# MLP "up" phases: the first group's plain halves and sums behind the copy of the second group's first product

## The chip, the cores and the metric

The kernel runs on one core of a Trainium2 chip. The metric is device time in microseconds for one execution. TensorE (PE) does the matmuls, VectorE (DVE) and ScalarE (ACT) the elementwise work, GpSimd (POOL) some elementwise work and accumulating DMAs, SyncE (SP) issues most loads.

## The reference

An encoder of two layers over 512 positions of width 1024: a stick-breaking attention, a squared-relu MLP, a gated linear recurrence, and a second MLP, each on a normed input and added to the stream. The change lies in both MLPs:

```python
def squared_relu_mlp(h, w1, w2):
    u = jax.nn.relu(h @ w1)
    return (u * u) @ w2          # w1: 1024 x 4096, w2: 4096 x 1024

x = x + squared_relu_mlp(rms_norm(x, norm_mlp[layer]), mlp_w1[layer], mlp_w2[layer])
```

## The kernel before, in words

Every matmul in full precision is made of three in a faster format: an operand is split into a high half (a cast, on ScalarE: `wh`, `bh`, `sh`) and a low half (operand minus high half, on VectorE: `wl`, `bl`, `sl`), and high by high, high by low and low by high are summed in PSUM.

The MLP is cut into four quarters of the hidden width. Each quarter is an "up" phase (input to hidden) and a "down" phase (hidden to output). Each phase multiplies 2 x 2 blocks by Strassen's scheme in Winograd's form: seven products `P1` to `P7` instead of eight, with sums of blocks before and after. The first quarter's up part is done directly (`squared`); the other three go through `run`, so `run` holds three up phases in each MLP, six in all.

An up phase has 14 steps of PE: the seven products for group `p = 0` and then the seven for `p = 1`, in the order P1 P5 P6 P3 P7 P2 P4 (`UP`). A group is one half of the quarter's hidden columns. P1, P6 and P7 add up in one PSUM bank, so the bank after P1 must be copied out before P6 may write it again; P5 and P3 share a second bank. After each step, `leave` writes the work on its product: copies of partial sums, combinations, relu and square. It also prepares operands of PE four steps ahead (`prepare`, `make`, `operand`): a cast `wh` and a subtraction `wl` for each weight block, and before some of them a sum `b` of two blocks, done on VectorE or by an accumulating DMA.

The hidden values of a group are four blocks, `u[0]` to `u[3]`. For the down phase they are needed as they are ("plain") and in four sums (`sums`), and each of these as halves (`split`). For group 0 the halves go to `bh` and `bl`; for group 1 to `sh` and `sl`. Plain halves of group 0 cover blocks 0 to 2 in one instruction of 1536 elements a partition; four `sums` of 512 elements overwrite the `u` blocks; the halves of the sums follow in two instructions of 1024.

ScalarE and VectorE execute this code in the order it is written: each is wrapped in `Ordered`, which ties every instruction to the one before it. Line 765 of the profile is the line of that wrapper, so instructions have to be told apart by their tiles. PE's order is written by hand as well. DMA queues are placed by the scheduler.

Of the kernel before, what the change touches and what calls it, by code (L numbers as in the profile page):

```python
# [61 lines left out]
def hybrid_encoder(  # L62
# [712 lines left out]
    class Mlp:  # L775
# [333 lines left out]
        def run(self, first, between, end):  # L1109
# [13 lines left out]
            def place(i):  # L1123

                return (i + self.STEPS // 2) % self.STEPS
# [35 lines left out]
            def prepare(i):  # L1161

                if i < len(steps) and steps[i][0] == "up":

                    if steps[i][3] == "P7" or self.layer and steps[i][1:] == (1, 0, "P4"):
                        return
                if i - 1 in range(len(steps)) and i - 1 not in made and i > 2:
                    make(i - 1)
                if i < len(steps) and steps[i][0] == "down":
                    add(i, 0)  # L1170
                    if waiting and place(i) in (20, 22, 23):
                        self.split_slot(*waiting.pop(0))
                make(i)
                for n in range(i + 1, i + 6):
                    add(n, n - i)

            def last_sums(u, which):
                for to, a, b, how in which:
                    self.V.tensor_tensor(u[to], u[a], u[b], how)
# [23 lines left out]
            def leave(i):  # L1203

                ahead = i + 4
                if i < 0:
                    return
                kind, q4, p, name = steps[i]
                bank = sums[kind, q4, p if kind == "up" else 0][self.PRODUCTS[name][3]]
                if kind == "down":  # L1210
                    if p:
                        for n in range(2):
                            self.collect(name, n, bank[n])
                    prepare(ahead)
                    if q4 == 0:

                        k = {19: 2, 20: 2, 24: 3, 25: 3}.get(place(i))
                        if k:
                            (self.sums_of_x if place(i) in (19, 24) else self.halves_of_sums)(k)
                        if place(i) == 26:  # L1220
                            self.replace()
                    return
                u, three = us[p], bank.rearrange("p (i n) -> p i n", i=2)
                keep = {"P1": 0, "P6": 1, "P5": 2, "P7": 3}.get(name)
                if keep is not None:

                    self.A.copy(u[keep], three)
                at, x, y, op = {
                    "P3": (1, three, u[1], ALU.subtract),
                    "P7": (2, u[2], u[3], ALU.subtract),  # L1230
                    "P2": (0, u[0], three, ALU.add),
                    "P4": (3, three, None, None),
                }.get(name, (None,) * 4)
                if op:
                    self.V.tensor_tensor(u[at], x, y, op)
                if name == "P4":
                    self.A.activation(u[3], three, AF.Relu)
                    self.square(u[3])
                    if p:
                        last_sums(u, self.SUMS[:2])  # L1240
                if later:
                    later.pop()()
                prepare(ahead)
                if op:
                    def rest(u=u, at=at):
                        self.A.activation(u[at], u[at], AF.Relu)
                        self.square(u[at])
                        if p:
                            self.split_slot(p, u[at], at)

                    if p and name == "P3":
                        later.append(rest)
                    else:
                        rest()
                    if name == "P2" and not p:
                        self.split(p, slice(0, 2), slice(0, 3), slice(0, 3))
                elif name == "P4" and p:
                    last_sums(u, self.SUMS[2:3])
                    self.split_slot(p, u[2], 5)
                    last_sums(u, self.SUMS[3:])  # L1260
                    waiting[:] = [(p, u[j], 3 + j) for j in (0, 1, 3)]
                elif name == "P4":
                    self.sums(p, slice(0, 2))
                elif name in ("P5", "P6") and p:
                    n = ("P5", "P6").index(name)
                    self.split(0, n, slice(0, 4), slice(3, 7))
# [16 lines left out]
            for i, (kind, q4, g, name) in enumerate(steps):  # L1283
                load(i)
                leave(i - 1)
                if i == len(steps) - 2:
                    break
                if kind == "down":
                    self.part(sums.setdefault((kind, q4, 0), {}), name, g, ws.pop(i))
                    continue  # L1290
                if name == "P1":
                    us[g] = self.slots_of(g)
                banks = sums.setdefault((kind, q4, g), {})
                to = self.PRODUCTS[name][3]
                new = to not in banks
                if new:
                    banks[to] = self.bank()
                self.up(name, ws.pop(i), banks[to], new)
# [492 lines left out]
```

## Time and profile before

| | |
|---|---|
| runs | 1038.54, 1039.32, 1039.6 us; median 1039.32 |
| profiled execution | 1039.46 us, of which the span of instructions is 1037.8 |
| PE | 1026.1 us busy, 99% |
| VectorE | 858.9 us, 83% |
| ScalarE | 701.8 us, 68% |
| GpSimd | 172.3 us, 17% |
| granted TensorE clock | 0.998 |

Times in rows of the profile are us from the start of the span: start, duration, engine, line, operation, what is written and read. `[1.48 <-ACT bh L765]` at the end of a row says that the engine was idle for 1.48 us before it, until the instruction named ended. Consecutive rows of one engine overlap by some 0.1 us, since a row ends when its last write is acknowledged. The six up phases run through `run` begin at 329, 407, 485, 796, 876 and 954 us; one takes some 39 us, as does a down phase.

### The profile page before, as it was taken

Reading aid. Unit: us, or ns where it says so; the run is one execution under the profiler, and the core shown is the slowest. Engines: PE = TensorE matmul, PEld = TensorE weight load, DVE = VectorE, ACT = ScalarE, POOL = GpSimd, SP = SyncE. Lnnn points to the kernel's source line nnn. Section 1 sums busy time; section 2 is a strip of 40 time slices with the busy share of each in tenths; the row PEclk is TensorE's granted clock in tenths of the full one; section 3 lists DMA queues with packets and bytes.
Section 4 is the critical chain, followed back from the end, with each engine's and each line's share of the span. In section 5 each row is a group of like instructions: output and inputs, shape, how many; then the busy total and the mean of one; then the engine's idle time right before and its main releaser. Section 6 shows DMA issues by size and latency. Waiting matters only on the chain.

```text
span 1037.8 us, 15857 instructions
## 1 busy us (share of the span) xinstructions
PE 1026.1 (99%) x5862; PEld 897.0 (86%) x5862; DVE 858.9 (83%) x1148; ACT 701.8 (68%) x1083; POOL 172.3 (17%) x239
## 2 busy tenths in 40 slices
PE   9999999999999999999999999999999999999997
PEld 7888888888888988988988888888888988988986
DVE  6888787847888898898899888984789798898897
ACT  6777676826766773773775799964755773873866
POOL 0444344420010010010011121200010010010013
PEclk9999999999999999999999999999999999999999
DMA  7745454528546677667682575462446677677654
GB/s 238 214 120 143 115 152 103 160 91 294 142 78 189 185 134 206 172 132 208 163 206 79 151 191 144 102 223 87 96 73 177 176 146 198 161 149 196 159 123 111
DMA packets 53260, 160.46 MB, mean 155 GB/s; under 512 B 6720, under 2 KB 8256, under 8 KB 53184
## 3 DMA queue, kind: packets, MB, share of 16 engines
q1 hardware_dynamic: 42096, 120.35, 35.4%
q0 software_dynamic: 10656, 38.80, 23.1%
q8 instruction: 46, 0.75, 0.3%
q10 hardware_dynamic: 432, 0.31, 0.1%
q14 instruction: 30, 0.25, 0.1%
HBM read 137.41 MB, written 4.19 MB: 136 GB/s over the span
## 4 chain that ended last, share of the span: by engine, by line
PE 74%; DVE 10%; issue 7%; ACT 5%; DMA 3%; POOL 0%; POOLq 0%; DVEq 0%; ACTq 0%
PE ps_t L1071 10%; PE ps_acc L1071 5%; PE ps_acc L231 5%; PE ps_acc L229 5%; PE ps_acc L230 5%; PE ps_acc L976 5%; DVE wl L765 4%; PE ps_z L976 4%; PE ps_t L229 2%; PE ps_t L231 2%; PE ps_t L230 2%; PE ps_z L1071 2%; ACT wh L765 2%; PE ps_o L976 2%; PE ps_o L229 2%
## 5 line engine op out<-in xcount | busy, mean ns | idle before, releaser
L765 ACT CAST wh<-b 128x1024 fp32r<-128x1024 f32 x168 | 174.2, 1049 | 125.0 <-DVE b L765 77.6
L765 DVE TENSOR_TENSOR wl<-b,wh 128x1024 fp32r<-128x1024 f32 x168 | 203.7, 1220 | 46.8 <-ACT wh L765 46.4
L1053 POOL DMA_DIRECT2D b<-in_w_dn x40 | 35.0, 874 | 364.5 <-DVE b L765 269.9
L229 PE MATMUL ps_acc<-xgh,wh 128*128 128x512 f32 x192 | 78.5, 409 | 0.0
L231 PE MATMUL ps_acc<-xgl,wh 128*128 128x512 f32 x192 | 75.2, 392 | 0.0
L230 PE MATMUL ps_acc<-xgh,wl 128*128 128x512 f32 x192 | 75.1, 391 | 0.0
L224 DVE TENSOR_TENSOR wl<-raw,wh 128x512 fp32r<-128x512 f32 (+2 forms) x70 | 62.0, 912 | 14.5 <-ACT wh L222 14.3
L589 DVE TENSOR_TENSOR_SCAN scan<-keep,later 128x128 f32<-128x128 f32 (+1 forms) x64 | 59.5, 934 | 17.0 <-ACT keep L579 11.5
L765 ACT ACTIVATE u<-u 128x512 f32<-128x512 f32 x100 | 63.1, 633 | 7.4 <-DVE u L765 5.9
L222 ACT CAST wh<-raw 128x512 fp32r<-128x512 f32 (+2 forms) x70 | 50.7, 759 | 20.8 <-PE ps_acc L231 7.3
L593 POOL TENSOR_TENSOR w<-w,scan 128x128 f32<-128x128 f32 (+1 forms) x64 | 51.7, 809 | 57.2 <-DVE scan L589 54.0
L1053 POOL DMA_DIRECT2D b<-in_w_up x24 | 20.8, 868 | 238.5 <-DVE b L765 71.2
L765 DVE TENSOR_TENSOR b<-b,b 128x1024 f32<-128x1024 f32 x48 | 58.7, 1223 | 1.3
L765 DVE TENSOR_TENSOR u<-u 128x512 f32<-128x512 f32 (+1 forms) x92 | 54.8, 596 | 2.7 <-ACT u L765 1.1
L765 ACT CAST wh<-raw 128x1024 fp32r<-128x1024 f32 x46 | 48.1, 1048 | 8.4 <-PE ps_acc L1071 8.3
L976 PE MATMUL ps_z<-xgh,wh 128*128 128x256 f32 x192 | 53.7, 280 | 0.0
L976 PE MATMUL ps_z<-xgh,wl 128*128 128x256 f32 x192 | 53.7, 280 | 0.0
L976 PE MATMUL ps_acc<-low,wh 128*128 128x256 f32 x192 | 53.6, 279 | 0.0
L1071 PE MATMUL ps_t<-wl,sh 128*128 128x512 f32 x126 | 49.8, 395 | 1.0 <-DVE wl L765 0.9
L1071 PE MATMUL ps_t<-wh,bh 128*128 128x512 f32 x126 | 49.2, 391 | 0.0
L1071 PE MATMUL ps_t<-wh,sl 128*128 128x512 f32 x126 | 49.2, 390 | 0.0
L1071 PE MATMUL ps_t<-wl,bh 128*128 128x512 f32 x126 | 49.1, 390 | 0.0
(399 smaller groups left out, 3416.7 us busy)
## 6 DMA issues: line engine op xcount, KB each, us to landing
b<-in_w_dn SPq DMA_DIRECT2D x48, 512.0 KB, 4.5
b<-in_w_dn POOLq DMA_DIRECT2D x40, 512.0 KB, 5.7
b<-in_w_up SPq DMA_DIRECT2D x36, 512.0 KB, 4.6
b<-in_w_up POOLq DMA_DIRECT2D x24, 512.0 KB, 5.6
raw<-in_w_m SPq DMA_DIRECT2D x16, 512.0 KB, 4.3
raw<-in_w_dn SPq DMA_DIRECT2D x16, 512.0 KB, 4.6
raw<-in_w_in SPq DMA_DIRECT2D x16, 512.0 KB, 3.8
raw<-in_w_qk SPq DMA_DIRECT2D x12, 512.0 KB, 3.6
```

Source lines behind the costliest of these rows:

```text
L222: A.copy(wh[:, k, :], raw[:, k, :])
L224: V.tensor_tensor(wl[:, k, :], raw[:, k, :], f(wh[:, k, :]), ALU.subtract)
L229: PE.matmul(ps, wh, ah, start=start, stop=False)
L230: PE.matmul(ps, wl, ah, start=False, stop=False)
L231: PE.matmul(ps, wh, al, start=False, stop=stop)
L589: V.tensor_tensor_scan(sc[:, S - n : S][:, ::-1], keep[:, :n][:, ::-1], later[:, S - n :][:, ::-1], 1.0, ALU.mult, ALU.max,)
L593: G.tensor_tensor(wt, wt, sc[:, S - n + 1 : S + 1], ALU.mult)
L765: ins = getattr(self.e, name)(*args, **kwargs)
L976: PE.matmul(ps[:, i * HS : (i + 1) * HS], m, y, start=new and i == k == n == 0, stop=i == 1 and k == C // 2 - 1 and n == 2, skip_group_che ...
L1053: G.dma_start(out=unit[b].rearrange("p j n -> p (j n)"), in_=unit["src"](to), accum_op=ALU.add)
L1071: PE.matmul(ps, m, y[:, jj, cols], start=first and n == 0, stop=last and n == 2, skip_group_check=not new,)
```

## The change

Two pieces of the work on group 0 are moved into `leave` for the first product of group 1. The plain halves (`split` of blocks 0 to 2, a cast on ScalarE and a subtraction on VectorE) stood behind relu and square of P2 of group 0, the sums behind P4 of group 0. Both now stand behind the copy of P1 of group 1.

```diff
                     else:
                         rest()
-                    if name == "P2" and not p:
-                        self.split(p, slice(0, 2), slice(0, 3), slice(0, 3))
                 elif name == "P4" and p:
...
                     waiting[:] = [(p, u[j], 3 + j) for j in (0, 1, 3)]
-                elif name == "P4":
-                    self.sums(p, slice(0, 2))
+                elif name == "P1" and p:
+                    self.split(0, slice(0, 2), slice(0, 3), slice(0, 3))
+                    self.sums(0, slice(0, 2))
                 elif name in ("P5", "P6") and p:
                     n = ("P5", "P6").index(name)
                     self.split(0, n, slice(0, 4), slice(3, 7))
```

ScalarE's order, in the first of the six up phases, from the weight half before group 0's relu of P2 to the weight half for P7 of group 1. `u<-ps_acc` is the relu of P4 of group 0, the next row its square, `wh<-b_3785` a weight for P3, `u<-ps_z` the copy of P1 of group 1 and `u<-ps_o` that of its P5:

```order
 L765 CAST wh<-b_3729 128x1024
 L765 ACTIVATE u<-u 128x2x256 x2
+L765 ACTIVATE u<-ps_acc 128x2x256
+L765 ACTIVATE u<-u 128x2x256
+L765 CAST wh<-b_3785 128x1024
+L765 COPY u<-ps_z 128x512
 L765 CAST bh<-u 128x2x768
-L765 ACTIVATE u<-ps_acc 128x2x256
-L765 ACTIVATE u<-u 128x2x256
-L765 CAST wh<-b_3785 128x1024
-L765 COPY u<-ps_z 128x512
 L765 COPY u<-ps_o 128x512
```

The cast `bh` has moved behind four instructions, to between the copies of P1 and P5.

VectorE's order at the same place. `u<-u,ps_z` is the combination for P2 of group 0, `wl<-b_3785` the low half of the weight for P3 of group 1, `u<-u x4` the four sums, `wl<-b_3783` the low half for P7 of group 1:

```order
 L765 TENSOR_TENSOR u<-u,ps_z 128x2x256
 L765 TENSOR_TENSOR wl<-b_3729,wh 128x1024
+L765 TENSOR_TENSOR wl<-b_3785,wh 128x1024
 L765 TENSOR_TENSOR bl<-u,bh 128x2x768
-L765 TENSOR_TENSOR wl<-b_3785,wh 128x1024
 L765 TENSOR_TENSOR u<-u 128x2x256 x4
 L765 TENSOR_TENSOR wl<-b_3783,wh 128x1024
```

The subtraction `bl` has moved behind one `wl`; the sums stand where they stood in the row. The other five up phases show the same two exchanges.

## The prediction

> **What bounds the kernel now.** I read the page first, then the waits of TensorE (PE), then the timeline of ScalarE (ACT) and VectorE (DVE) around one of the six places that the change touches, then PE's rows there. Two lines of the page and PE's longest waits:
>
> ```profile
> PE 1026.1 (99%) x5862; PEld 897.0 (86%) x5862; DVE 858.9 (83%) x1148; ACT 701.8 (68%) x1083; POOL 172.3 (17%) x239
> b<-in_w_dn POOLq DMA_DIRECT2D x40, 512.0 KB, 5.7
> ...
> PE ps_z L976 <- ACT u L765: 1.5, 1, 1.5
> PE ps_t L1071 <- DVE wl L765: 0.9, 3, 0.5
> ```
>
> PE is busy for 99% of the span, so there is little to win: its two longest sorts of wait in the MLPs together are 2.4 us. The question is therefore whether PE has to wait for something new. One of its waits, 1.5 us for the copy `u` on ScalarE, lies at the place of the change; the three for `wl`, the low half of a weight block, lie half a phase later.
>
> The change acts once in each of six "up" phases (three quarters after the first, in two MLPs). ScalarE there, in the first of them:
>
> ```profile
> 349.01 1.29 ACT L765 ACTIVATE u<-u 128x512 f32<-128x512 f32 x2
> 350.33 1.48 ACT L765 CAST bh<-u 128x1536 fp32r<-128x1536 f32 x1
> 351.72 0.59 ACT L765 ACTIVATE u<-ps_acc 128x512 f32<-128x512 f32 x1
> 352.34 0.63 ACT L765 ACTIVATE u<-u 128x512 f32<-128x512 f32 x1
> 352.88 1.03 ACT L765 CAST wh<-b 128x1024 fp32r<-128x1024 f32 x1
> 353.81 0.58 ACT L765 COPY u<-ps_z 128x512 f32<-128x512 f32 x1
> 354.84 0.59 ACT L765 COPY u<-ps_o 128x512 f32<-128x512 f32 x1 [0.45 <-PE ps_o L976]
> 355.33 1.05 ACT L765 CAST wh<-b 128x1024 fp32r<-128x1024 f32 x1
> ```
>
> In order: relu and square of P2; `bh`, the high plain halves of the first group (the cast that moves); relu and square of P4; a weight's high half; the copy of the second group's P1 (ps_z), then of its P5 (ps_o). VectorE beside it:
>
> ```profile
> 349.14 1.23 DVE L765 TENSOR_TENSOR wl<-b,wh 128x1024 fp32r<-128x1024 f32 x1 [0.57 <-ACT wh L765]
> 351.84 1.76 DVE L765 TENSOR_TENSOR bl<-u,bh 128x1536 fp32r<-128x1536 f32 x1 [1.48 <-ACT bh L765]
> 353.94 1.23 DVE L765 TENSOR_TENSOR wl<-b,wh 128x1024 fp32r<-128x1024 f32 x1 [0.34 <-ACT wh L765]
> 355.08 2.86 DVE L765 TENSOR_TENSOR u<-u 128x512 f32<-128x512 f32 x4
> 357.86 1.22 DVE L765 TENSOR_TENSOR wl<-b,wh 128x1024 fp32r<-128x1024 f32 x1
> ```
>
> The reader is to see that VectorE stands idle twice before the four sums (1.48 and 0.34 us), and not at all behind them. How full it stays up to the down phase, and what its few waits there are:
>
> ```profile
> 358.00:386.00 28.00, 27.92 (x168) 24.68 (x168) 26.52 (x30) 20.29 (x28) 3.54 (x5) 1.00 0.68 150
> 365.39 1.23 DVE L765 TENSOR_TENSOR b<-b,b 128x1024 f32<-128x1024 f32 x1
> 366.65 1.05 ACT L765 CAST wh<-b 128x1024 fp32r<-128x1024 f32 x1 [0.44 <-DVE b L765]
> 369.58 0.69 DVE L765 TENSOR_TENSOR sl<-u,sh 128x512 fp32r<-128x512 f32 x1 [0.62 <-ACT sh L765]
> 374.05 1.42 DVE L765 TENSOR_TENSOR u<-u 128x512 f32<-128x512 f32 x2 [0.18 <-ACT u L765]
> 383.22 2.00 ACT L765 CAST wh<-b 128x1024 fp32r<-128x1024 f32 x2 [5.33 <-DVE b L765]
> 384.30 2.36 DVE L765 TENSOR_TENSOR wl<-b,wh 128x1024 fp32r<-128x1024 f32 x2 [0.57 <-ACT wh L765]
> ```
>
> VectorE is busy for 26.52 of these 28 us. Of the 1.48 us left, 0.62, 0.18 and 0.57 are waits for ScalarE, which in turn had waited for VectorE's own sum `b` (0.44 and 5.33 us). Such waits are no slack: when VectorE comes later, ScalarE comes later, and the wait comes later with the same length. The chain ends at PE, on the second matmul of the down phase's P6, in five of the six phases:
>
> ```profile
> 351.82 0.28 PE L976 MATMUL ps_o<-s,wh 128*128 128x256 f32 x1
> 360.42 0.28 PE L976 MATMUL ps_z<-xgh,wl 128*128 128x256 f32 x1
> ...
> 385.12 0.39 PE L1071 MATMUL ps_t<-wh,sh 128*128 128x512 f32 x1
> 385.59 0.50 PE L1071 MATMUL ps_t<-wl,sh 128*128 128x512 f32 x1
> 463.27 0.50 PE L1071 MATMUL ps_t<-wl,sh 128*128 128x512 f32 x1 [0.17 <-DVE wl L765]
> 541.50 0.51 PE L1071 MATMUL ps_t<-wl,sh 128*128 128x512 f32 x1 [0.51 <-DVE wl L765]
> 822.85 0.38 PE L976 MATMUL ps_z<-bh,wh 128*128 128x256 f32 x1 [1.49 <-ACT u L765]
> 854.00 0.50 PE L1071 MATMUL ps_t<-wl,sh 128*128 128x512 f32 x1 [0.25 <-DVE wl L765]
> ...
> 928.90 0.39 PE L1071 MATMUL ps_t<-wh,bh 128*128 128x512 f32 x1
> 931.62 0.39 PE L1071 MATMUL ps_t<-wh,sh 128*128 128x512 f32 x1
> 931.95 0.50 PE L1071 MATMUL ps_t<-wl,sh 128*128 128x512 f32 x1
> ```
>
> Undisturbed, the 12 matmuls of this shape in a step take 2.72 us (928.90 to 931.62), 0.23 us each. Here the second one comes 0.47 us behind the first at 385.59 and 0.33 at 931.95, and three rows name `wl` outright. So PE takes this low half as soon as it is there: the slack is nought in these five, and I assume it nought in the sixth, whose down phase has another order. That is what decides my forecast: PE looks saturated, but through this stretch VectorE sets its pace.
>
> **The change part by part.** *The cast `bh` goes behind the copy.* It removes 1.48 us ahead of the relu of P4, so relu, square, weight half and copy begin earlier. The relu needs nothing of the cast; allowing for the overlap of neighbours of about 0.1 us (351.84 less 351.72 against a cast that ends at 351.81), it starts near 350.22. From the rows' starts: relu to square 0.62, square to `wh` 0.54, `wh` to copy 0.93. The copy starts at 352.31, 1.50 us earlier than at 353.81. The product is ready for it: the next product, P5 into ps_o, began at 351.82, so P1's last matmul began 0.12 us before and ended, with 0.28 us, near 351.98. PE's P6, which adds to that bank, may then start sooner. The list of PE's waits has one there in all six phases, the 1.49 us at 822.85.
>
> *The subtraction `bl` goes behind one `wl`.* VectorE's row order changes by that one exchange; the four sums stand where they stood, between the same neighbours, since no weight is prepared between the two places in the code. But they now follow `bl` directly, and they overwrite what `bl` reads. Their start: copy 352.31, plus 0.49 (a copy to its neighbour, 354.84 to 355.33) gives the cast at 352.80; plus 1.51 (350.33 to 351.84) gives `bl` at 354.31; plus its 1.76 and 0.02 for the hand-over gives the sums at 356.09. Before, they began at 355.08. **They begin 1.01 us later**: the copy has been put into the chain (0.49), and `bl` stands in it (1.78) in place of a `wl` (1.14) and of waits that fell away. The work that could hide this is the idle time behind the sums, and there is none but the waits that move along. So `wl` for P7, P2, P4 and those of the down phase all come 1.01 us later.
>
> *At PE.* In the first phase P7 wants its `wl` at 360.42; it now ends at 357.86 + 1.22 + 1.01 = 360.09, still in time. Further on the margin is used up, until at 385.59 it is nought, and the whole 1.01 us is PE's. PE then leads by nothing and VectorE catches up behind P6, where PE's row of waits shows none; so the next phase starts afresh and pays again. In the phase of 822.85 the wait of 1.49 goes, but the wait at 854.00 shows that PE is held by `wl` later in the same phase all the same: the time saved at P6 is spent at P7, where the `wl` is a microsecond later and PE a microsecond and a half sooner. It pays 1.01 as well.
>
> *Price of the copy by a page.* The Trainium skill, "ScalarE: Activation LUTs" (What ACT_TABLE_LOAD costs), puts an ACTIVATE with immediate operands at 186 ns and 0.833 ns an element, overlapping by 93 ns with its neighbour. Taken over to this copy of 512, as an estimate, that is 0.52 us where the rows give 0.49; the sum would be 0.2 us longer by it.
>
> *DMAs.* The written order of SyncE's queue shifts a reload of `x` and a load of the final scale ahead of one weight load each, near the ends of the MLPs' last down phases; both are read much later, and I price that at nought. Loads and accumulating DMAs that follow a `wl` or `b` of this stretch are issued 1.01 us later too. Those of GpSimd land after 5.7 us in the page's row, and feed P7 and P4, the ends of their phase; I price them at nought, and up to 0.1 us for each phase if that cover were gone.
>
> **Sum.** Six phases by 1.01 us: 6.06 us. The profiled execution took 1039.46 us (1037.8 of span and 1.66 around it), 0.14 above the median of the runs, 1039.32. Its time becomes 1045.5, and the median **1045.4 us**. Bounds for a phase: 0.5 us, if half of a delay is caught up by waits that I call fixed; 1.35 us, with 0.11 for each of two or three further interrupted steps (the matmul behind an interrupted one is late by about that: 0.50 for its duration in the rows instead of 0.39) and the DMAs. Six times these are 3.0 and 8.1: 1042.3 to 1047.4.
>
> **Rivals.**
>
> *Faster: the wait for the copy is what counts.* The mechanism is the bank of the second group's P1, which P6 adds to. Copied 1.5 us earlier it takes away 822.85's 1.49 us, the restart of 0.1 to 0.2 behind it, and a few tenths in the others: 1.8 us, and 1037.5 us. It decides if VectorE can make good 1 us between 358 and 386. For it: it is PE's longest wait in the list. Against it: 26.52 of 28 us busy, and the five rows at P6. The Trainium skill, "PSUM — Partial Sum Buffer" (Summary: rules for kernel authors), says to evacuate promptly, which is what the change does and would make it faster by this amount. The trace bears out that a late copy stops PE, once in six.
>
> *Absorbed: VectorE catches up in part.* If the waits of 0.62, 0.18 and 0.57 us were slack after all, 1.37 us would cover the 1.01 in each phase, and only the gain of one wait and the odd interrupted step would be left: within a microsecond or two, 1038 to 1041. Against it: ScalarE's rows with their own waits on VectorE's `b`. If only some phases absorb, 1041 to 1043.
>
> *Slower still: later weights delay DMAs.* Were a load late by a full step (2.72 us) in one phase of each MLP, that adds 5.4 us: 1050.8. Against it: none of PE's longest waits in the list is on a DMA.
>
> *The change does nothing* is excluded by the orders of both engines, which differ at all six places.
>
> **How the numbers follow.** Forecast with its bounds, 0.82; absorbed in full or in part, 0.09, about half of it within 0.2% (2.1 us, about what a measurement of this kernel tells from no change); faster, 0.06; slower still, 0.03. The range 1042.3 to 1047.4 is the forecast's own, and leaves out the rivals, 0.18. Faster by over 0.2%: 0.06. Within: 0.06. Slower: 0.88.
>
> **What would show it.** Right: in the timeline of ScalarE the copy of the second group's P1 stands before `bh`. From the relu of P2 (349.01) to the sums (355.08) it is 6.07 us; this grows to 7.1 in all six phases. VectorE waits some 2.1 us for `wh` and then some 0.7 for `bh`, where it waited 1.48 and 0.34. PE's waits on `wl` grow from 0.9 us to several, at P6 of the down phases or somewhat before, and the wait on ACT `u` at P6 of the up phase is gone. Wrong: the sums 1 us later with PE's waits on `wl` unchanged (then there was slack), the sums no later (then the chain is mis-added), or new waits on DMAs.

## The result, and the profile after

| | before | after |
|---|---|---|
| median of 5 runs | 1039.38 us | 1044.47 us |
| lowest to highest | 1038.54 to 1040.47 | 1044.17 to 1044.77 |
| profiled execution (span) | 1039.46 (1037.8) | 1044.17 (1042.4) |

After to before is 1.0054, with an interval of 1.0043 to 1.0064: 5.1 us slower; the prediction was 1045.4 us, 6.1 more than the runs of before then shown. The granted clock is the same in both profiled executions, 0.998.

The page of after, its line of busy times, and then PE's two largest sorts of wait in the MLPs from the list of waits (total us, times, longest):

```profile
PE 1028.7 (99%) x5862; PEld 894.0 (86%) x5862; DVE 858.0 (82%) x1148; ACT 701.0 (67%) x1083; POOL 172.3 (17%) x239
...
PE ps_z L976 <- ACT u L765: 2.9, 4, 1.9
PE ps_t L1071 <- DVE wl L765: 1.1, 5, 0.3
```

None of these lines shows where 5 us went. PE's busy time grew by 2.6 us with the same 5862 matmuls, and the two sorts of wait grew by 1.6 us in all. PE's waits are spread over so many matmuls that few of them are listed (below, *Where PE lost it*). So the loss has to be read from starts, in the stretch that the change touches. ScalarE there, in the timeline of after:

```profile
348.07 1.29 ACT L765 ACTIVATE u<-u 128x512 f32<-128x512 f32 x2
...
351.35 0.58 ACT L765 COPY u<-ps_z 128x512 f32<-128x512 f32 x1
351.82 1.48 ACT L765 CAST bh<-u 128x1536 fp32r<-128x1536 f32 x1
```

The copy begins 3.28 us behind the relu of P2, where it was 4.80 (353.81 less 349.01). It is 1.52 us earlier; the prediction had 1.50. VectorE beside it:

```profile
348.19 1.23 DVE L765 TENSOR_TENSOR wl<-b,wh 128x1024 fp32r<-128x1024 f32 x1 [0.57 <-ACT wh L765]
351.47 1.22 DVE L765 TENSOR_TENSOR wl<-b,wh 128x1024 fp32r<-128x1024 f32 x1 [2.06 <-ACT wh L765]
353.33 1.76 DVE L765 TENSOR_TENSOR bl<-u,bh 128x1536 fp32r<-128x1536 f32 x1 [0.64 <-ACT bh L765]
355.13 2.87 DVE L765 TENSOR_TENSOR u<-u 128x512 f32<-128x512 f32 x4
```

VectorE now waits 2.06 us for the weight's `wh` and then 0.64 for `bh`, where it waited first 1.48 for `bh` and then 0.34 for `wh`. From the relu of P2 to the sums it is 7.06 us (355.13 less 348.07) against 6.07: 0.99 later, with 1.01 predicted. In the timelines of the other five phases it is 7.06 or 7.07, against 6.07 or 6.08. Behind the sums VectorE is as full as before, 26.53 us of 28, in the table of windows:

```profile
358.00:386.00 28.00, 27.75 (x162) 23.35 (x161) 26.53 (x30) 20.27 (x28) 3.49 (x5) 1.00 0.65 149
```

What a phase pays is the distance from one first matmul of P1 to the next. In the timeline of PE, the two that enclose the first of the six phases, of before and then of after:

```profile
329.14 0.28 PE L976 MATMUL ps_acc<-xgh,wh 128*128 128x256 f32 x1
407.26 0.28 PE L976 MATMUL ps_acc<-xgh,wh 128*128 128x256 f32 x1
```

```profile
328.34 0.28 PE L976 MATMUL ps_acc<-xgh,wh 128*128 128x256 f32 x1
407.31 0.28 PE L976 MATMUL ps_acc<-xgh,wh 128*128 128x256 f32 x1
```

That is 78.12 us before and 78.97 after, 0.85 longer, and this includes the down phase. The same subtraction for all six, for after and for the experiments that follow, against before's profiled execution (us). No P1 follows at once on phases 3 and 6: phase 3 ends here at the first matmul of the layer's next part, and phase 6 at the last matmul of the program.

| kernel | 1 | 2 | 3 | 4 | 5 | 6 | sum |
|---|---|---|---|---|---|---|---|
| after | 0.85 | 1.01 | 0.68 | 0.93 | 1.01 | 1.00 | 5.5 |
| e1, ahead of the copy | 0.39 | 0.52 | 0.20 | 0.80 | 0.54 | 0.53 | 3.0 |
| e2, subtraction alone | 1.66 | 1.81 | 1.48 | 2.04 | 1.85 | 1.78 | 10.6 |
| e3, halves of the sums later | 0.53 | 0.66 | 0.35 | 1.07 | 0.66 | 0.66 | 3.9 |
| e4, one subtraction less | -0.27 | -0.13 | -0.43 | 0.29 | -0.13 | -0.02 | -0.7 |
| e5, weight behind the copy | -0.34 | -0.18 | -0.37 | -0.34 | -0.07 | -0.14 | -1.4 |
| e6, halves cut in two | -0.37 | -0.59 | -1.18 | -1.22 | -0.24 | -0.32 | -3.9 |

So the loss is spread over the six places, 0.7 to 1.0 us at each. In after, the stretch ahead of the first P1 was 0.80 us shorter (328.34 for 329.14). No edit touches that stretch, and over the eight kernels of this document it ends between 327.59 and 329.14. The 5.5 less this 0.8 is the 4.7 by which the profiled execution is longer.

The column of phase 4 holds something else besides. VectorE's combination for P2 (`u<-u,ps_z`) stands ahead of all that the change, and e1 to e5, move. In phases 2, 3, 5 and 6 it starts equally far behind the phase's first matmul in all of these kernels, to within 0.02 us. In phase 4 it starts 20.50 us behind it in before, but 20.44 in after, 20.76 in e1, 20.72 in e2, 20.94 in e3, 20.90 in e4 and 20.38 in e5; why was not looked into. With these differences to before taken off, phase 4 reads 0.99, 0.54, 1.82, 0.63, -0.11 and -0.22, like the other phases.

### The profile page after: what moved, and what is told of

Same layout as the page of the kernel before. It is cut to its first block, busy times and chain, and to the rows that moved or that the text cites. A ratio compares the mean times of both kernels' runs of the same rounds, so it can differ in the third digit from the quotient of the medians.

```text
span 1042.4 us, 15858 instructions
## 1 busy us (share of the span) xinstructions
PE 1028.7 (99%) x5862; PEld 894.0 (86%) x5862; DVE 858.0 (82%) x1148; ACT 701.0 (67%) x1083; POOL 172.3 (17%) x239
## 4 chain that ended last, share of the span: by engine, by line
PE 75%; DVE 12%; ACT 7%; issue 4%; DMA 2%; SPq 0%; POOL 0%; DVEq 0%; ACTq 0%; POOLq 0%
PE ps_t L1071 10%; PE ps_acc L976 8%; PE ps_acc L1071 5%; PE ps_acc L229 5%; PE ps_acc L231 5%; PE ps_acc L230 5%; PE ps_z L976 5%; DVE wl L765 4%; PE ps_o L976 3%; ACT wh L765 2%; PE ps_z L1071 2%; PE ps_t L230 2%; PE ps_t L229 2%; PE ps_t L231 2%; ACT u L765 2%
```

## The experiments

The theory: through these phases VectorE sets PE's pace. A phase costs what the change adds to VectorE's chain from the relu of P2 to the sums, whatever PE's waits on ScalarE do. The main rival: the waits of PE, for the copies on ScalarE above all, set the time. Beside e1 to e4 the kernel before had a median of 1038.72 us, and beside e5 and e6 one of 1038.69 (15 runs each); the ratios are to these.

### e1: plain halves and sums ahead of the copy

On after, the two pieces go behind the first group's P4 instead, so that the cast `bh` stands ahead of the copy. `bl` and the sums stay one behind the other.

```diff
-                elif name == "P1" and p:
-                    self.split(0, slice(0, 2), slice(0, 3), slice(0, 3))
-                    self.sums(0, slice(0, 2))
+                elif name == "P4":
+                    self.split(p, slice(0, 2), slice(0, 3), slice(0, 3))
+                    self.sums(p, slice(0, 2))
```

> Plain halves and sums of group 0 behind P4's relu, square and weight, but still ahead of the copy of P1. VectorE's order is that of the changed kernel; on ScalarE only the copy is not in the chain. Chain theory (the later start of the four sums is paid by PE in each of six phases): sums start 0.49 us earlier than in the changed kernel, 0.52 later than before; 6 x 0.52 = 3.1 us over the kernel before, about 1042.5. Rival (what costs is the place of the halves behind the second group's first product): the time of the kernel before, 1039.4. Rival (VectorE's exchange costs it all): the time of the changed kernel, 1044.5.

Measured: 1042.13 us; ratio to before 1.0036 [1.0023, 1.0049], and by phases 3.0 us in all. VectorE, in the timeline of e1:

```profile
348.28 1.23 DVE L765 TENSOR_TENSOR wl<-b,wh 128x1024 fp32r<-128x1024 f32 x1 [0.57 <-ACT wh L765]
...
352.94 1.76 DVE L765 TENSOR_TENSOR bl<-u,bh 128x1536 fp32r<-128x1536 f32 x1 [0.16 <-ACT bh L765]
354.74 2.87 DVE L765 TENSOR_TENSOR u<-u 128x512 f32<-128x512 f32 x4
```

The wait for `bh` fell from 0.64 to 0.16. Counted from the `wl` ahead of it, the sums begin 6.46 us later; in before it is 5.94 (355.08 less 349.14) and in after 6.94 (355.13 less 348.19). So the copy in the chain is worth 0.48 us, and `bl` behind the weight the other 0.52. The six phases follow with 0.50 each on average. The two halves of the predicted microsecond are real, and of about the sizes that it gave them (0.49 and 0.52).

### e2: the subtraction moved, the cast left where it was

Here `bh` stays ahead of the relu of P4, as in before; `bl` and the sums go behind the copy. The edit is shown against before.

```diff
                     if name == "P2" and not p:
-                        self.split(p, slice(0, 2), slice(0, 3), slice(0, 3))
+                        h = self.places(p)[0][:, slice(0, 2), slice(0, 3), :]
+                        self.A.copy(h, self.u[p][:, slice(0, 2), slice(0, 3), :])
...
-                elif name == "P4":
-                    self.sums(p, slice(0, 2))
+                elif name == "P1" and p:
+                    a = slice(0, 2), slice(0, 3)
+                    h, l = (t[:, a[0], a[1], :] for t in self.places(0))
+                    self.ready = self.V.tensor_tensor(
+                        l, self.u[0][:, a[0], a[1], :], f(h), ALU.subtract
+                    )
+                    self.sums(0, slice(0, 2))
```

> Only the subtraction bl and the sums move behind P1's copy in the written order; the cast bh stays behind P2. ScalarE's order is that of the kernel before, VectorE's that of the changed one. Chain theory: bl now waits for wl of P3 to end its slot (355.08 in the trace before) and the sums follow 1.78 us later: 6 x 1.78 = 10.7 us over the kernel before, about 1050. Rival (ScalarE's order is what PE feels): the time of the kernel before, 1039.4. The wait on the copy at P6 of the fourth phase stays at 1.5 us or more by either.

Measured: 1049.9 us; 1.0111 [1.0096, 1.0126]. VectorE, in the timeline of e2:

```profile
348.63 1.23 DVE L765 TENSOR_TENSOR wl<-b,wh 128x1024 fp32r<-128x1024 f32 x1 [0.57 <-ACT wh L765]
353.44 1.22 DVE L765 TENSOR_TENSOR wl<-b,wh 128x1024 fp32r<-128x1024 f32 x1 [3.58 <-ACT wh L765]
354.58 1.75 DVE L765 TENSOR_TENSOR bl<-u,bh 128x1536 fp32r<-128x1536 f32 x1
356.36 2.87 DVE L765 TENSOR_TENSOR u<-u 128x512 f32<-128x512 f32 x4
```

All of VectorE's idle time now lies ahead of the weight (3.58 us), and nothing of `bl` is covered. From `wl` to the sums it is 7.73 us, 1.79 more than before; the phases pay 1.77 each on average. One half of the change thus costs twice what the whole costs: moving the cast too lets the weight's `wh` come earlier on ScalarE, and so wins back 0.8 us of the 1.8. e2 alone does not exclude the rival, though: in its list, PE's waits for the copies on ScalarE in `ps_z` rose to 7.7 us (7 times), from 1.5 in before. Which of the two is the cause is decided by e4.

### e3: the halves of the sums one step later

On after, the halves of the four sums go behind the steps P6 and P3 of the second group, instead of P5 and P6. The copy of P6 then no longer stands behind the first of their casts on ScalarE.

```diff
-                elif name in ("P5", "P6") and p:
-                    n = ("P5", "P6").index(name)
+                if name in ("P6", "P3") and p:
+                    n = ("P6", "P3").index(name)
```

> The changed kernel with the halves of the sums (two casts, two subtractions) one product later each, behind P6 and P3 of group 1 instead of P5 and P6. In the changed kernel PE waits at P7 for the copy of P6, which stands on ScalarE behind the cast of the first sums (2.9 us in four waits named). If that wait is a cost of its own, it goes and the time falls by 1 to 3 us, to 1041.5 to 1043.5. If VectorE's lateness sets the end of each phase whatever happens at P7, the wait goes, the waits for wl in the down phase grow by as much, and the time stays within 1 us of 1044.5.

To see why this was tried: in after, PE has a new wait at P7, the third product to add to the shared bank. There are four of these, in phases 2, 3, 4 and 6. In the timeline of PE in after, here are the first and the longest of them, with P6 of phase four between:

```profile
438.29 0.38 PE L976 MATMUL ps_z<-xgh,wh 128*128 128x256 f32 x1 [0.33 <-ACT u L765]
...
823.00 0.39 PE L976 MATMUL ps_z<-bh,wh 128*128 128x256 f32 x1
830.64 0.39 PE L976 MATMUL ps_z<-xgh,wh 128*128 128x256 f32 x1 [1.92 <-ACT u L765]
```

And what VectorE and ScalarE did ahead of 830.64, in their timelines:

```profile
826.15 2.87 DVE L765 TENSOR_TENSOR u<-u 128x512 f32<-128x512 f32 x4
829.05 1.04 ACT L765 CAST bh<-u 128x1024 fp32r<-128x1024 f32 x1 [2.35 <-DVE u L765]
830.01 0.58 ACT L765 COPY u<-ps_z 128x512 f32<-128x512 f32 x1
```

The four sums end on VectorE at 829.02; the cast of their halves waits for them for 2.35 us, and the copy that PE wants is queued behind that cast. P6 of the same phase (823.00) waits for nothing any more. So the wait of 1.49 us for the copy of P1 has become one of 1.92 for the copy of P6.

Measured: 1042.71 us; 1.0037 [1.0023, 1.0051], and 3.9 us by phases, where after had 5.5. PE's longest waits in e3:

```profile
PE ps_z L976 <- DVE wl L765: 1.4, 1, 1.4
...
PE ps_z L976 <- ACT u L765: 0.4, 1, 0.4
```

By its time alone this lies in the range that was expected if the wait is a cost of its own, and outside the other. The phases tell it otherwise. The waits on the copy fell from 2.9 to 0.4 us, and 1.92 of them had stood in phase four. Yet phase four gained no more than the others: it reads 1.07 against 0.93 as measured, and 0.63 against 0.99 without the later start of VectorE, 0.36 less, and PE waits 1.4 us for `wl` there instead. The other five phases gained 0.32 to 0.35 each, also those (1 and 5) with no listed wait on the copy at P7. So the wait on the copy cost nothing of its own. One row of VectorE shows where that came from, in the timeline of after and then of e3:

```profile
369.63 0.69 DVE L765 TENSOR_TENSOR sl<-u,sh 128x512 fp32r<-128x512 f32 x1 [0.62 <-ACT sh L765]
```

```profile
366.13 1.22 DVE L765 TENSOR_TENSOR bl<-u,bh 128x1024 fp32r<-128x1024 f32 x1
...
369.97 0.69 DVE L765 TENSOR_TENSOR sl<-u,sh 128x512 fp32r<-128x512 f32 x1 [0.28 <-ACT sh L765]
```

The wait for `sh` shrank from 0.62 to 0.28 us, by the same 0.34; it reads 0.62 in after and 0.28 in e3 in all six phases. The second `bl` of the sums, which stood further ahead, now stands between the weight sum `b`, for which ScalarE waits, and the `sl` that waits for ScalarE. The phases became shorter because work was put where VectorE stood idle.

### e4: one subtraction less behind the sums

On after, the low halves of the second half of the sums are left out (they keep older data): an instruction of 1.22 us less on VectorE in each phase, 1.13 from its start to that of the next, and nothing less on PE or ScalarE.

```diff
-                    self.split(0, n, slice(0, 4), slice(3, 7))
+                    if n == 0:
+                        self.split(0, n, slice(0, 4), slice(3, 7))
+                    else:
+                        self.A.copy(self.places(0)[0][:, n, 3:7, :], self.u[0][:, n, 0:4, :])
```

> The changed kernel without the low halves of the second half of the sums: one subtraction of 1024 elements less on VectorE in each phase (those low halves keep older data), ScalarE's order and PE's work unchanged. Chain theory: VectorE is 1.13 us earlier behind it in all six phases, more than the 1.01 lost; the waits for wl in the down phase fall to those of before or less, and the time to 1039 to 1040. Rival (ScalarE's copies set PE's pace): no change, 1044.5, since no copy comes earlier.

Measured: 1039.17 us; 1.0005 [0.9996, 1.0015], the time of before. Against after the phases are 1.12, 1.14, 1.11, 0.64, 1.14 and 1.02 us shorter. The first entry in PE's list of waits in e4:

```profile
PE ps_z L976 <- ACT u L765: 3.2, 5, 1.9
```

The waits on `wl` are gone from the list, and those on the copies are as large as in after (3.2 us against 2.9). With all of the waits on ScalarE still there, the whole loss is gone: VectorE's chain was the loss. In phase four the copy still holds PE for 1.9 us, and the gain reads only 0.64; but VectorE started 0.46 later there than in after (20.90 for 20.44), ahead of the edit, and with that it is 1.10. So this wait, the largest in the list, cost nothing here either.

### e5: a weight behind the copy, instead of the halves

On before, the opposite order: the weight for P3 goes behind the copy, and `bl` and the sums stay ahead of it and follow each other directly.

```diff
-                prepare(ahead)
+                if name == "P1" and p:
+                    prepare(ahead - 1)
+                if name != "P4" or p:
+                    prepare(ahead)
```

> The kernel before, with halves and sums of group 0 in their old places; instead the weight for P3 of group 1 (its cast and its subtraction) goes behind the copy of P1. So the copy comes 0.93 us earlier, as the change meant it to, and the four sums follow bl at once (353.62 instead of 355.08 in the trace before), with the weight's subtraction behind them. Chain theory: the weight for P7 ends 0.32 us earlier, and the wait at P6 of the fourth phase shrinks from 1.5 to some 0.6 us; PE's waits for wl in the down phases fall, six times by up to 0.3: 0.7 to 1.9 us less than before, 1037.0 to 1038.3 beside 1039. Rival (an early copy is of no use, since PE's waits only move on): no change within 0.5 us. Rival on the slow side: P3's weight now ends within 0.1 us of PE's need and stops PE in every phase, up to 0.3 us each, 1.8 us more.

Measured: 1037.53 us; 0.9987 [0.9978, 0.9995]. VectorE, in the timeline of e5, and then one row from that of before:

```profile
348.76 1.23 DVE L765 TENSOR_TENSOR wl<-b,wh 128x1024 fp32r<-128x1024 f32 x1 [0.57 <-ACT wh L765]
...
353.33 2.87 DVE L765 TENSOR_TENSOR u<-u 128x512 f32<-128x512 f32 x4
...
358.39 1.22 DVE L765 TENSOR_TENSOR wl<-raw,wh 128x1024 fp32r<-128x1024 f32 x1
```

```profile
358.99 1.22 DVE L765 TENSOR_TENSOR wl<-raw,wh 128x1024 fp32r<-128x1024 f32 x1
```

and PE's longest wait in its list of waits:

```profile
PE ps_o L976 <- DVE wl L765: 1.6, 3, 1.2
```

The sums begin 1.37 us earlier (4.57 behind the `wl`, against 5.94), but a phase gains only 0.24 on average. The reason is that the weight's subtraction, which stood ahead of the sums, now stands behind them. The first row that both kernels have at the same place again is `wl<-raw`, and it comes 9.63 us behind the first `wl` (358.39 less 348.76), against 9.85 in before (358.99 less 349.14). VectorE's chain is thus 0.22 us shorter, and the phases gain that much, as the chain theory expects. The weight that was moved back is late in three of PE's steps (1.6 us in phases 2, 4 and 6), but this did not make these phases longer than before: they too gained 0.14 to 0.34.

### e6: the plain halves cut in two

On e5's edit, blocks 1 and 2 of the plain halves go behind P7 of the first group, where VectorE waited, and block 0 stays behind P2. The sums go ahead of the weights of that step.

```diff
                     if p:
                         last_sums(u, self.SUMS[:2])
+                    else:
+                        self.sums(p, slice(0, 2))
...
+                    if name == "P7" and not p:
+                        self.split(p, slice(0, 2), slice(1, 3), slice(1, 3))
                     if name == "P2" and not p:
-                        self.split(p, slice(0, 2), slice(0, 3), slice(0, 3))
+                        self.split(p, slice(0, 2), slice(0, 1), slice(0, 1))
...
-                elif name == "P4":
-                    self.sums(p, slice(0, 2))
```

> As the run with the weight behind the copy, and the plain halves are cut in two: blocks 1 and 2 right behind P7 of group 0, where they are ready, block 0 behind P2. The cast between P2's square and P4's relu is then 256 x 2 elements instead of 768 x 2 (about 0.6 us for 1.48), the subtraction 0.69 for 1.76; one instruction more on each engine. Chain theory: the sums start another microsecond earlier, more than PE's remaining waits for wl are worth, so these vanish: 2 to 3 us less than before, 1036 to 1037 beside 1039. Rival (the two instructions more in front of P2 delay P2's own work): no better than the run without the cut.

Measured: 1035.27 us; 0.9964 [0.9951, 0.9978], 3.4 us faster than before, a little more than expected, and the fastest of the kernels here. VectorE, in the timeline of e6:

```profile
347.50 1.22 DVE L765 TENSOR_TENSOR bl<-u,bh 128x1024 fp32r<-128x1024 f32 x1
...
351.34 0.69 DVE L765 TENSOR_TENSOR bl<-u,bh 128x512 fp32r<-128x512 f32 x1 [0.89 <-ACT bh L765]
352.50 2.87 DVE L765 TENSOR_TENSOR u<-u 128x512 f32<-128x512 f32 x4 [0.47 <-ACT u L765]
```

Two thirds of the subtraction stand ahead of the `wl` now, which fills the 0.57 us for which VectorE waited there, and the last third takes 0.69 us instead of 1.76. The sums begin 23.61 us behind the phase's first matmul, at 328.89, where it was 25.94 in before (355.08 less 329.14). Phases 3 and 4 gained most (1.18 and 1.22), the others 0.24 to 0.59. Some 0.3 of phase 3 is a disturbance of before (below, *The sum, mis-sized*).

This time the phase does not gain all of VectorE's lead. At P6 of the down phase VectorE's two `wl` start at 383.06, which is 54.17 us behind the phase's first matmul, where it was 55.16 in before (384.30 less 329.14): 0.99 earlier, and the phase gained 0.37. The lead ends behind P6, where ScalarE waits for PE before its next cast. In the timeline of before and then of e6:

```profile
388.42 1.05 ACT L765 CAST wh<-b 128x1024 fp32r<-128x1024 f32 x1 [0.25 <-PE ps_t L1071]
```

```profile
387.79 1.06 ACT L765 CAST wh<-b 128x1024 fp32r<-128x1024 f32 x1 [0.86 <-PE ps_t L1071]
```

PE itself is no longer held there: P6 and the step behind it take 5.45 us together in e6, two undisturbed steps of 2.72, where they took 5.82 in before and 5.98 in after. In phases 2, 3 and 5 of e6 it is 5.43 or 5.44. In phase 4 it is still 5.74, so PE is held there yet, and the lead is gained in full: the two `wl` come 1.25 us earlier (55.68 for 56.93), and the phase gained 1.22.

## Why the prediction was right

*The copy earlier, the sums later.* Both terms came out to within 0.02 us in the first phase (1.52 for 1.50; 0.99 for 1.01), and so did VectorE's two waits (2.06 and 0.64, with "some 2.1" and "some 0.7" predicted). e1 splits the microsecond into the copy, 0.48, and the rest, 0.52. e2 shows the part that an undivided look at the diff would have got wrong: without the cast, the same move costs 1.77 a phase.

*VectorE sets the pace.* e1, e2 and after put 0.52, 1.79 and 1.00 us into VectorE's chain ahead of the sums, and the phases grew by 0.50, 1.77 and 0.92 on average. e4 took 1.13 us out behind the sums, and with PE's waits on ScalarE as large as in after the loss was gone. e5 made the chain 0.22 us shorter and the phases gained 0.24. The rival "Faster: the wait for the copy is what counts" falls with that. PE's list of waits had its largest entry exactly where the change helped, and without it phase four still paid 0.93 of the 1.01 us, or 0.99 without the offset of its start. The Trainium skill's rule to evacuate promptly ("PSUM — Partial Sum Buffer", Summary: rules for kernel authors), which stood beside that rival, is not contradicted as far as the wait goes, since 822.85's did vanish with the earlier copy. It was no guide to the time here: the copy came 1.5 us sooner and the kernel took 5.1 us more.

*At PE, the wrong name.* The step said that the time saved at P6 of phase four "is spent at P7, where the `wl` is a microsecond later". The place was right and the cause listed there was not: PE's wait of 1.92 us at 830.64 is for the copy of P6, which stands behind the cast of the sums' halves and so behind the sums themselves. The step had followed only the weights behind the sums, and not what ScalarE has queued behind them. The amount came out all the same (0.93 for 1.01), since the late sums hold the `wl` as well: with that wait removed, in e3, PE waited 1.4 us for `wl` instead.

*Where PE lost it.* PE waits on `wl` at P6 of five down phases, as predicted, but for 0.21 to 0.25 us each (1.1 in all), and not for "several". The rest was lost in pieces too small for the list. In the timeline of PE in after, the first matmuls of three successive steps of the first down phase, and then the second matmul of P6:

```profile
376.41 0.40 PE L1071 MATMUL ps_z<-wh,bh 128*128 128x512 f32 x1
379.35 0.39 PE L1071 MATMUL ps_acc<-wh,sh 128*128 128x512 f32 x1
382.28 0.39 PE L1071 MATMUL ps_t<-wh,bh 128*128 128x512 f32 x1
...
385.64 0.50 PE L1071 MATMUL ps_t<-wl,sh 128*128 128x512 f32 x1 [0.25 <-DVE wl L765]
```

From one to the next it is 2.94 and 2.93 us, where before took 2.72 for each (376.96 to 379.68 to 382.40), without a wait being named. The step ahead of them takes 3.04 for 2.72, and P6 with the step behind it 5.98 for 5.82. Together that is 0.91, which is the loss of this phase (0.85) to within 0.1. The statement that PE is late for `wl` somewhat before P6 holds; the list was the wrong place to see its size. The sixth phase, for which it was only assumed that there is no slack, paid 1.00.

*The sum, mis-sized.* 6.06 us was forecast, six times 1.01; the phases measure 5.5. Phases 2, 5 and 6 paid 1.00 or 1.01, but phase 1 paid 0.85 and phase 3 0.68. The term is right for what the change adds; what failed is taking six equal phases from one profiled execution of before, in which two were disturbed and a third a little. In phase 1 it was VectorE's combination for P2, in the timelines of before and of after:

```profile
347.89 0.68 DVE L765 TENSOR_TENSOR u<-u,ps_z 128x512 f32<-128x512 f32 x1
```

```profile
346.94 0.68 DVE L765 TENSOR_TENSOR u<-u,ps_z 128x512 f32<-128x512 f32 x1
```

It begins 18.75 us behind the phase's first matmul in before (347.89 less 329.14) and 18.60 in after (346.94 less 328.34), so before's phase was 0.15 late ahead of anything that the change touches; 0.15 and 0.85 are 1.00. In phase 3 it was an accumulating DMA. ScalarE and VectorE, in the timeline of before:

```profile
534.28 1.05 ACT L765 CAST wh<-b 128x1024 fp32r<-128x1024 f32 x1 [2.20 <-DMA b<-in_w_dn]
...
533.98 1.22 DVE L765 TENSOR_TENSOR wl<-b,wh 128x1024 fp32r<-128x1024 f32 x1
535.37 1.23 DVE L765 TENSOR_TENSOR wl<-b,wh 128x1024 fp32r<-128x1024 f32 x1 [0.17 <-ACT wh L765]
536.51 0.75 DVE L765 SCALAR_TENSOR_TENSOR c<-ps_t,rr,c 128x512 f32<-128x512 f32 x1
```

and VectorE at the same place in after:

```profile
536.04 2.35 DVE L765 TENSOR_TENSOR wl<-b,wh 128x1024 fp32r<-128x1024 f32 x2
538.31 0.74 DVE L765 SCALAR_TENSOR_TENSOR c<-ps_t,rr,c 128x512 f32<-128x512 f32 x1
```

The late DMA held ScalarE for 2.20 us, and VectorE's three instructions took 2.53 us from the start of the first to that of the last in before, against 2.27 in after: 0.26 of the missing 0.33. The same two phases lie low by much the same amounts in e1 and e2 (by 0.1 to 0.2 in phase 1, by 0.3 in phase 3, against phases 2, 5 and 6), as they must if the offset belongs to before's execution. Less than 0.1 us of phase 3 stays open. In phase 4 the 0.06 us by which VectorE started later in before makes 0.99 of the 0.93.

*Waits that are "no slack".* The prediction called VectorE's waits of 0.62, 0.18 and 0.57 us behind the sums fixed, so that nothing could be absorbed. For this change that held: the 0.62 stands in after unaltered, at 369.63. As a statement on the kernel it was too strong: other work can be put into such a wait, and e3 won 0.34 us in five phases so.

*Which way the kernel is balanced.* Longer chains on VectorE are paid in full (e1, e2, after), and a chain shorter by 0.22 us was gained nearly in full (e5). A lead of 0.99 us was not: in e6 the first phase kept 0.37 of it, and PE's steps at P6 were undisturbed again. So VectorE sets the pace of the kernel before, but in most phases by a few tenths of a microsecond only; past that PE's own matmuls bound the down phase.

## What to carry to other kernels

PE was busy for 99% of the span here, and another engine paced it. So price a reordering by what it adds to the chain on the engine that never catches up, up to the first instruction that stands at the same place in both orders, and not by how early one piece becomes, nor by the largest entry in the list of waits. In e5 the sums came 1.37 us earlier, and the phase gained the 0.22 by which that next row was earlier. That entry can vanish, or move to the next instruction in the same queue, without the time following it. When something must go behind an early copy, choose the piece that nothing long follows, and put the rest where the pacing engine already waits: here the same place with a weight instead of the halves gave a ratio of 0.9987 (e5), and with the halves cut in two besides 0.9964 (e6).

## What the runs showed of the hardware

The same matmul step runs at two rates while the granted clock reads 0.998. In the timeline of PE in after, the first matmuls of two steps and of the steps behind them, each step being 24 matmuls of 256 columns:

```profile
423.76 0.28 PE L976 MATMUL ps_acc<-xgh,wh 128*128 128x256 f32 x1
426.48 0.28 PE L976 MATMUL ps_z<-xgh,wh 128*128 128x256 f32 x1
...
429.32 0.28 PE L976 MATMUL ps_o<-s,wh 128*128 128x256 f32 x1
432.14 0.28 PE L976 MATMUL ps_z<-bh,wh 128*128 128x256 f32 x1
```

The first pair is 2.72 us apart and the second 2.82, with no wait in either. The slower rate holds for several steps; a step takes 2.72 again from 441.13 on, behind the step that had waited 0.33 us at 438.29. Its cause is open. It bears on how much PE could gain where VectorE does not pace it, about 0.1 us a step; the loss of this change was read from VectorE's chain and does not rest on it.

The accumulating DMAs on GpSimd's queue land after 5.7 us at the median, but in before three of them in a row, issued from 522.7 to 529.3 us, took between 7.7 and 9.2 us. One of these is the late operand at 534.28. In after, that wait was absent.
